# Seven of eight block products in half of the output projection of a two-layer decoder

## Chip, core and metric

One of the eight cores of a Trainium2 chip runs the whole program. The metric is device microseconds for one execution. A core has a matrix engine (TensorE, PE in the profile), three engines for elementwise work (VectorE or DVE, ScalarE or ACT, GpSimd or POOL) and a queue engine, SyncE (SP), which issues all DMAs of this kernel. Each engine works its own instruction list strictly in order and waits there for the others.

## What is computed

Two decoder layers on 1024 tokens with 1024 features, in float32, then a final norm. Cut to what matters here:

```python
def reference(x, ...):
    for l in range(2):
        h = rmsnorm(x, norm1[l])
        qa, ka, va, qb, kb, vb, gate_pre = split(h @ w_in[l])
        o_a = dilated_mixture(qa, ka, va)           # 12 heads of windowed attention
        o_b = stick_breaking_attention(qb, kb, vb)  # 4 heads
        gates = sigmoid(gate_pre + b_gate[l])
        merged = g_a * (o_a @ w_br[l, :256]) + g_b * (o_b @ w_br[l, 256:])
        x = x + merged @ w_o[l]                     # the output projection
        h2 = rmsnorm(x, norm2[l])
        a, v = split(h2 @ w_up[l])                  # 2 x 2816 columns
        a = causal_depthwise_conv(a, conv_w[l], conv_b[l])
        x = x + (gelu(a) * v) @ w_down[l]
    return rmsnorm(x, norm_f)
```

The stick-breaking attention takes for each query the product, over later keys, of (1 - sigmoid): a running product along a row of up to 1024 keys, which the kernel makes with a scan on DVE.

## The kernel before

**Layout and precision.** Activations lie with features on the 128 partitions and tokens along the free axis; the tokens come in two halves of 512, n = 0 and 1, the features in eight chunks of 128, e or k = 0 to 7. To keep float32 accuracy each operand is held as two numbers, hi and lo (`split`: ACT casts hi, L131, DVE subtracts to get lo, L136), and every block product is three matmuls: hi x hi, hi x lo, lo x hi. `product` (L163 to L165) does so for a whole chunk over eight k: 24 matmuls of 512 columns.

**Seven products.** The FFN's up and down projections, and the gates and far-attention inputs of the mixer, are already done in pairs of chunks by Winograd's form of Strassen's scheme: the input is a 2 by 2 grid of blocks (token half by feature half), the weights of two output chunks another, and seven block products of 12 matmuls (`seven`, L921 to L923) take the place of eight. It needs four sums of input blocks, S[1] to S[4], each split into hi and lo, and four sums of weight blocks per pair. For the mixer these come from `block_sums`, a list of small steps put between other work (`dense.side`), each of which waits for a named event such as "N01s".

**Order.** PE's order is that of the program text, written by hand through generators: a unit yields after a few matmuls, and `drive(side, main, ratio, lead)` runs `lead` steps of main and then `ratio` steps of main for each step of side. The other engines' orders and the DMA queue's are made by a planner from priorities and estimated times: it may pull an instruction ahead of its place in the text when its inputs and its buffer are there, and raises those in `tc.high_priority`. The buffers are named by tags: `ql` (2), `p4` (4), `e8` (6), `wr` (2, raw weights), `wh` and `wl` (4 each, split weights), `ot` (1), `pt` (6 of 512 columns).

**Around the change.** In the mixer stick-breaking items come first. `score` computes a row block, ACT takes two sigmoids of it, and `scans` runs the scan over the whole row (L651) and a multiplication (L654); it is called after each `turn`, which transposes 128-blocks on PE (L667) and splits them into `sbh` and `sbl`, read by `apply` (L679). The near items follow (`p0h`, `p0l`, L743), then the far items, with the pairs of `pair` between them. Then comes the branch loop: 16 steps over (n, e), each with two products of `product` into `br_ps`, a multiplication by the gate (L1297), their sum `mrg` (L1302), which `merged` writes into H[n] as hi (ACT) and lo (POOL). In the first layer this loop also transposes x into the residual (`residual_in`). The gates are loaded by `gate_in` (`gin`), the branch weights by `branch_in` through `wr`. Before this loop `next(wo[0])` loads and splits the weights of the first output chunk, through `wr` as well.

The output projection itself is 16 units `wo_chunk(l, n, e)`, all eight e for n = 0, then all for n = 1. Each loads its own weights, runs `product` into `o_ps`, adds the result to x (L1136) and its squares to the norm's sum (`norm_add`, L424, L426). `relay` makes each unit's weights ready one unit ahead. `drive(first_half(), relay(*wo, primed=True), 2.5, 36)` puts the second norm of half 0 (sums L473, factors L482, `hh` and `hl` L487 to L490) and the FFN's first input sum (`first_sum`, L463) between the chunks of n = 1. The norm of half 1 runs between the first products of the FFN (`u_ps`).

Of the kernel before, what the change touches and what calls it, by code (L numbers as in the profile page):

```python
# [56 lines left out]
def trunk_kernel(ctx, tc, x, norm1, w_in, b_gate, w_br, w_o, norm2, w_up, conv_w, conv_b, w_down, norm_f, out, depth=None, probe=None):  # L57
# [341 lines left out]
    def xc(n, e, sub=slice(0, HF)):  # L399
        return X[n][e // 4][:, e % 4, sub]  # L400
# [15 lines left out]

    def norm_add(n, e, first=False, sub=slice(0, HF), adds=None):

        if first:
            ACC[n] = sb.tile([P, HF], F32, tag="ql", bufs=2, name="nrm")  # L420
        acc = ACC[n]
        acc = acc[:, sub]
        sq = acc if first else small("sq")[:, sub]
        act.activation(sq, xc(n, e, sub), AF.Square)  # L424
        if not first:
            (adds or (dve if e % 3 == 1 else pool)).tensor_tensor(acc, acc, sq, ALU.add)  # L426
# [193 lines left out]
    def stick_item(pr, s, qp):  # L620
# [6 lines left out]
        def score(a):  # L627
# [6 lines left out]
            for c0 in range(0, L, 512):  # L634
# [3 lines left out]
                with tc.high_priority(offset=AHEAD):  # L638
# [3 lines left out]
                    act.activation(sv[:, c0 : c0 + w], z[:, :w], AF.Sigmoid, scale=-1.0)  # L642
            SCANS.append((bt, sv, L))
            if L <= 512:
                scans()

        def scans():

            for bt, sv, L in SCANS:
                rev = sv[:, 0:L][:, ::-1]  # L650
                one = dve.tensor_tensor_scan(rev, rev, zero[:, 0:1].to_broadcast([P, L]), 1.0, ALU.mult, ALU.add)  # L651
# [9 lines left out]
        def turn(kb):  # L661
# [6 lines left out]
            shared[kb] = parts(tp, len(todo) * P, "sb")  # L668
            scans()

# [256 lines left out]
    def block_sums():  # L927
# [16 lines left out]
        def further(t, a, i):  # L944
            if t == 4:

                S[4] = half(0, 0)
            elif i == 0:
                new_s(t)
            r, (ah, al) = keep["r"][:, i, :], a()[i]  # L950
# [33 lines left out]
    def pair(dense, l, offs, tiled, put):  # L984
# [29 lines left out]
        yield  # L1014
        pool.tensor_tensor(a11, a12, a11, ALU.subtract)
        yield
# [101 lines left out]
    def gate(l, c):  # L1118
# [4 lines left out]
        for n in range(2):  # L1123
# [5 lines left out]
            yield  # L1129

    def wo_chunk(l, n, e):
# [4 lines left out]
        dve.tensor_tensor(xc(n, e), xc(n, e), o, ALU.add)  # L1136
        norm_add(n, e, e == 0)
        yield

    def residual_in():  # L1140

        for n in range(2):
            for c in range(0 if n else 1, 4):
                xr = sb.tile([P, T], F32, tag="ql", bufs=2, name="xr")
                t0 = n * HF + c * P
# [8 lines left out]
    def mixer(l, pending):  # L1154
# [123 lines left out]
        for i, ab in order:  # L1278
# [23 lines left out]
            dve.tensor_tensor(m, gt[:, 0, :], gt[:, 1, :], ALU.add)  # L1302
            late.append((n, e, m))
            if len(late) > 1:
# [643 lines left out]
```

## Time and profile before

| | us |
|---|---|
| median of 3 runs (2694.21 to 2697.93) | 2696.02 |
| the profiled execution | 2700.21 |
| its span, first to last instruction | 2698.4 |
| PE busy | 2662.5 |
| DVE busy | 2017.0 |
| ACT busy | 1352.6 |
| POOL busy | 672.1 |
| mean granted TensorE clock | 0.997 |

The span is that of one execution; its own time is 1.8 us longer. Matmuls overlap in the array, so a busy PE says that it is never without a matmul, not how many it starts: that is seen in the number of instructions in a window. In the rows a time in brackets is the idle time of that engine ahead of the instruction, with what ended it. In the rows of windows each engine has its busy time and its count, and behind them stand the granted clock, the share of the DMA engines and GB/s.

### The profile page before, as it was taken

Reading aid. Unit: us, or ns where it says so; the run is one execution under the profiler, and the core shown is the slowest. Engines: PE = TensorE matmul, PEld = TensorE weight load, DVE = VectorE, ACT = ScalarE, POOL = GpSimd, SP = SyncE. Lnnn points to the kernel's source line nnn. Section 1 sums busy time; section 2 is a strip of 40 time slices with the busy share of each in tenths; the row PEclk is TensorE's granted clock in tenths of the full one; section 3 lists DMA queues with packets and bytes.
Section 4 is the critical chain, followed back from the end, with each engine's and each line's share of the span. In section 5 each row is a group of like instructions: output and inputs, shape, how many; then the busy total and the mean of one; then the engine's idle time right before and its main releaser. Section 6 shows DMA issues by size and latency. Waiting matters only on the chain.

```text
span 2698.4 us, 36609 instructions
## 1 busy us (share of the span) xinstructions
PE 2662.5 (99%) x13104; PEld 2233.0 (83%) x13104; DVE 2017.0 (75%) x2974; ACT 1352.6 (50%) x2494; POOL 672.1 (25%) x487
## 2 busy tenths in 40 slices
PE   9999999999999999999999999999999999999999
PEld 8988888878888888888888888888788888888888
DVE  5776855675788888897657777566858888898865
ACT  5655645474455555532435565455645555554225
POOL 1003221122233444321210042211211443343210
PEclk9999999999999999999999999999999999999999
DMA  5012178663234444688411122785732444446863
GB/s 161 28 56 85 57 189 247 199 231 105 82 124 166 146 151 150 222 319 319 161 36 43 48 79 87 210 247 177 233 89 76 156 156 141 164 149 252 330 248 120
DMA packets 358689, 421.03 MB, mean 156 GB/s; under 512 B 20732, under 2 KB 287340, under 8 KB 356972
## 3 DMA queue, kind: packets, MB, share of 16 engines
q1 hardware_dynamic: 358508, 418.70, 47.0%
q8 instruction: 103, 1.69, 0.3%
q14 instruction: 78, 0.64, 0.1%
HBM read 278.59 MB, written 140.05 MB: 155 GB/s over the span
## 4 chain that ended last, share of the span: by engine, by line
PE 84%; DVE 8%; issue 2%; ACT 2%; DMA 2%; POOL 0%; SPq 0%; DVEq 0%; ACTq 0%; POOLq 0%
PE u_a L921 5%; PE u_a L922 5%; PE u_a L923 5%; PE d_ps L1644 5%; PE d_ps L1645 5%; PE d_ps L1646 5%; PE u_c L921 3%; PE u_c L922 3%; PE u_c L923 3%; PE i_a L921 2%; PE i_a L922 2%; PE i_a L923 2%; PE o_ps L163 2%; PE o_ps L164 2%; PE o_ps L165 2%
## 5 line engine op out<-in xcount | busy, mean ns | idle before, releaser
L136 DVE TENSOR_TENSOR w_lo<-up_a,w_hi 128x512 fp32r<-128x512 f32 x240 | 237.6, 996 | 20.6 <-ACT w_hi L131 20.6
L131 ACT CAST w_hi<-up_a 128x512 fp32r<-128x512 f32 x240 | 149.3, 622 | 184.1 <-PE u_a L922 45.3
L1652 DVE TENSOR_TENSOR x<-x,d_ps 128x512 f32<-128x512 f32 (+1 forms) x228 | 151.8, 671 | 76.6 <-PE d_ps L1646 75.3
L1383 POOL TENSOR_TENSOR cv<-cv 128x512 f32<-128x512 f32 x88 | 132.3, 1515 | 249.3 <-DVE cv L1378 139.5
L136 DVE TENSOR_TENSOR w_lo<-w_raw,w_hi 128x512 fp32r<-128x512 f32 x148 | 111.6, 757 | 61.9 <-ACT w_hi L131 61.3
L136 DVE TENSOR_TENSOR g<-cv,g 128x512 fp32r<-128x512 f32 x154 | 152.6, 992 | 5.2 <-ACT g L131 2.7
L131 ACT CAST w_hi<-w_raw 128x512 fp32r<-128x512 f32 x148 | 91.9, 621 | 125.3 <-PE o_ps L164 64.3
L131 ACT CAST w_hi<-in_a 128x512 fp32r<-128x512 f32 x120 | 74.6, 621 | 121.1 <-PE i_c L922 53.6
L136 DVE TENSOR_TENSOR w_lo<-in_a,w_hi 128x512 fp32r<-128x512 f32 x120 | 86.8, 723 | 61.9 <-ACT w_hi L131 61.5
L1644 PE MATMUL d_ps<-gd_in,w_hi 128*128 128x512 f32 (+1 forms) x340 | 130.4, 384 | 1.7 <-issue 0.9
L1646 PE MATMUL d_ps<-gd_in,w_lo 128*128 128x512 f32 (+1 forms) x340 | 129.8, 382 | 0.0
L1645 PE MATMUL d_ps<-gd_in,w_hi 128*128 128x512 f32 (+1 forms) x340 | 129.8, 382 | 0.0
L921 PE MATMUL u_a<-hh,w_hi 128*128 128x512 f32 x320 | 124.6, 389 | 0.8 <-DVE u L1534 0.8
L922 PE MATMUL u_a<-t_lo,w_hi 128*128 128x512 f32 x320 | 124.5, 389 | 0.0
L922 PE MATMUL u_a<-hl,w_hi 128*128 128x512 f32 x320 | 124.5, 389 | 0.0
L923 PE MATMUL u_a<-hh,w_lo 128*128 128x512 f32 x320 | 124.5, 389 | 0.0
L921 PE MATMUL u_a<-t_hi,w_hi 128*128 128x512 f32 x320 | 124.5, 389 | 0.0
L923 PE MATMUL u_a<-t_hi,w_lo 128*128 128x512 f32 x320 | 124.5, 389 | 0.0
L1644 PE MATMUL d_ps<-gd_in,wd 128*128 128x512 f32 (+1 forms) x292 | 113.9, 390 | 0.0
L131 ACT CAST g<-cv 128x512 fp32r<-128x512 f32 x154 | 94.9, 616 | 37.2 <-POOL cv L1383 29.9
L1646 PE MATMUL d_ps<-gd_in,wd 128*128 128x512 f32 (+1 forms) x292 | 112.8, 386 | 0.0
L1645 PE MATMUL d_ps<-gd_in,wd 128*128 128x512 f32 (+1 forms) x292 | 112.8, 386 | 0.0
(404 smaller groups left out, 8606.7 us busy)
## 6 DMA issues: line engine op xcount, KB each, us to landing
gd<-g SPq DMA_DIRECT2D x154, 512.0 KB, 3.7
gd_in<-gd SPq DMA_DIRECT2D x154, 512.0 KB, 5.9
up_a<-in_w_up_dram SPq DMA_DIRECT2D x80, 512.0 KB, 4.9
t_kq<-tk SPq DMA_DIRECT2D x32, 768.0 KB, 4.7
wd_raw<-in_w_down_dram SPq DMA_DIRECT2D x22, 1024.0 KB, 11.8
w_raw<-in_w_in_dram SPq DMA_DIRECT2D x80, 256.0 KB, 3.0
in_a<-in_w_in_dram SPq DMA_DIRECT2D x40, 512.0 KB, 5.4
gin<-gs SPq DMA_DIRECT2D x32, 512.0 KB, 4.1
```

The costliest lines, as they stand in the source:

```text
L131: one = act.copy(hi, src)
L136: two = dve.tensor_tensor(lo, src, f32(hi), ALU.subtract)
L163: pe.matmul(o, lh, rh, start=(first and i == 0), stop=False, skip_group_check=share)
L164: pe.matmul(o, lh, rl, start=False, stop=False, skip_group_check=share)
L921: pe.matmul(o, w[0][:, c], rh, start=(first and i == 0), stop=False, skip_group_check=True)
L922: pe.matmul(o, w[0][:, c], rl, start=False, stop=False, skip_group_check=True)
L923: pe.matmul(o, w[1][:, c], rh, start=False, stop=(last and i == 3), skip_group_check=True)
L1383: return lambda: pool.tensor_tensor(dst, a, b, ALU.subtract)
L1644: pe.matmul(o[:, sub], wh[:, c], gh[:, sub], start=(i == 0 and k in (0, 4, 5)), stop=False, skip_group_check=True)
L1645: pe.matmul(o[:, sub], wh[:, c], gl[:, sub], start=False, stop=False, skip_group_check=True)
L1646: pe.matmul(o[:, sub], wl[:, c], gh[:, sub], start=False, stop=(i == m - 1), skip_group_check=True)
L1652: dve.tensor_tensor(x, x, o[:, sub], ALU.add)
```

## The change

Output chunks 0 to 3 are computed in two pairs, (0, 1) and (2, 3), for both halves at once with seven block products (`wo_pair`); chunks 4 to 7 stay plain. The order is: chunks 4 to 7 of half 0, the two pairs, chunks 4 to 7 of half 1. The four input sums of the merged branches are made by `merged_sums`: the first, r = m(0, e) - m(1, e), on POOL in the branch loop, S[1], S[2] and S[3] with DVE and ACT, S[4] with POOL and ACT in the place of H[0]'s first half. `wo_all` sets them between the steps of the chunks by a count of steps, and makes each unit's weights ready during the one before. The second norm of half 0 now runs between the four plain chunks of half 1 (lead 44, ratio 1.2).

The first chunk's weights are loaded at step i == 12 of the branch loop instead of ahead of it. The scans of the stick-breaking rows go in pieces of at most 512 columns, from the end of the row to its start, each beginning with the last value of the one before; after a turn all but two of the waiting pieces are done, at least one. In `block_sums` the subtraction of b22 moves from the series after "N11s" to one after "N01s". In `pair` the difference a12 - a11 moves from POOL to DVE. x tiles of the first layer's residual go alternately to `ot` and `ql`, and the norm's sums to `ot` (half 1) and `p4` (half 0).

```diff
-        def scans():
-            for bt, sv, L in SCANS:
-                rev = sv[:, 0:L][:, ::-1]
-                one = dve.tensor_tensor_scan(rev, rev, zero..., 1.0, ALU.mult, ALU.add)
+            for c1 in range(L, 0, -512):
+                SCANS.append((bt, sv, max(0, c1 - 512), c1, L))
+        def scans(most=9):
+            while SCANS and most:
+                most -= 1
+                bt, sv, c0, c1, L = SCANS.pop(0)
+                rev = sv[:, c0:c1][:, ::-1]
+                one = dve.tensor_tensor_scan(rev, rev, zero..., 1.0 if c1 == L else sv[:, c1 : c1 + 1], ALU.mult, ALU.add)
...
-                dve.tensor_tensor(bt[:, 0 : L - 1], bt[:, 0 : L - 1], sv[:, 1:L], ALU.mult)
-            SCANS.clear()
+                k0, k1 = max(0, c0 - 1), c1 - 1
+                dve.tensor_tensor(bt[:, k0:k1], bt[:, k0:k1], sv[:, k0 + 1 : k1 + 1], ALU.mult)
...
-            scans()
+            scans(max(1, len(SCANS) - 2))
...
-        series({"N11s"}, 2, lambda i: further(2, b22, i), 1, 1)
+        for i in range(4):
+            todo.append(({"N01s"}, lambda i=i: less(b22, i)))
+        series({"N11s"}, 2, lambda i: i or new_s(2), 0, 1)
...
-        pool.tensor_tensor(a11, a12, a11, ALU.subtract)
+        dve.tensor_tensor(a11, a12, a11, ALU.subtract)
...
+    def wo_pair(l, e):
+        def put(c, n, x):
+            wo_add(n, e + c, x, n == 1 and e + c == 0)
...
+        u1, u2 = u[:, HF:T], u[:, 0:HF]
+        with tc.high_priority(offset=AHEAD):
+            pool.tensor_tensor(u2, a11, a21, ALU.subtract)
+            SUMS.append(pool.tensor_tensor(a21, a21, a22, ALU.add).ins.name)
+        yield
+        w1 = piece(a11)
+        yield
+        w2 = piece(a12)
+        yield
+        dve.tensor_tensor(a11, a21, a11, ALU.subtract)
+        w6 = piece(a11)
+        yield
+        w5 = piece(a21)
+        yield
+        pool.tensor_tensor(a11, a12, a11, ALU.subtract)
...
+        yield from seven(pa, w1, half(1, 0), True, True)
+        act.copy(u1, pa)
+        w7 = piece(u2)
+        yield
+        yield from seven(pb, w2, half(1, 1), True, True)
+        dve.tensor_tensor(u1, u1, pb, ALU.add)
+        put(0, 1, u1)
+        w3 = piece(a11)
+        yield
+        yield from seven(pa, w6, S[2], False, True)
...
+        yield from seven(pc, w5, S[1], True, True)
+        act.copy(u5, pc)
+        w4 = piece(a22)
...
+        yield from seven(pa, w7, S[3], False, True)
+        dve.tensor_tensor(u5, u5, pa, ALU.add)
+        put(1, 0, u5)
...
+        yield from seven(pc, w3, half(0, 1), False, True)
+        dve.tensor_tensor(u2, u2, pc, ALU.add)
+        put(0, 0, u2)
...
+        for word in seven(pa, w4, S[4], False, True):
+            yield "turn"
+            yield
+        put(1, 1, pa)
...
+    def merged_sums(r):
+        b12, b21, b22 = half(0, 0), half(1, 1), half(0, 1)
...
+        def s1(i):
+            split(*S[1][i], r[:, i, :])
+        def s2(i):
+            dve.tensor_tensor(r[:, i, :], f32(b22[i][0]), r[:, i, :], ALU.subtract)
+            dve.tensor_tensor(r[:, i, :], r[:, i, :], f32(b22[i][1]), ALU.add)
+            split(*S[2][i], r[:, i, :])
+        def s3(i):
+            t = small("s3")
+            dve.tensor_tensor(t, f32(b22[i][1]), f32(b12[i][1]), ALU.subtract)
+            dve.tensor_tensor(t, t, f32(b22[i][0]), ALU.add)
+            dve.tensor_tensor(t, t, f32(b12[i][0]), ALU.subtract)
+            split(*S[3][i], t)
+        def s4(i):
+            one = pool.tensor_tensor(r[:, i, :], f32(b21[i][0]), r[:, i, :], ALU.subtract)
+            tc.add_manual_dep(one.ins, SUMS[-1], NO_SYNC, reason="behind the sums of weights")
+            pool.tensor_tensor(r[:, i, :], r[:, i, :], f32(b21[i][1]), ALU.add)
+        def s4_parts(i):
+            act.copy(S[4][i][0], r[:, i, :])
+            pool.tensor_tensor(S[4][i][1], r[:, i, :], f32(S[4][i][0]), ALU.subtract)
+        for i in range(4):
+            at(i, lambda i=i: s1(i))
+            at(4 + i, lambda i=i: s2(i))
+            at(14 + 2 * i, lambda i=i: s3(i))
+            at(16 + 2 * i, lambda i=i: s4(i))
+            at(23 + i, lambda i=i: s4_parts(i))
...
-        wo = [wo_chunk(l, n, e) for n in range(2) for e in range(KD)]
+        wo = [(wo_chunk(l, 0, e), 1) for e in range(4, KD)] + [(wo_pair(l, e), READY) for e in (0, 2)]
+        wo += [(wo_chunk(l, 1, e), 1) for e in range(4, KD)]
...
-        next(wo[0])
         next(residual, None)
...
+                    pool.tensor_tensor(r1[0][:, e, :], mrg.pop((0, e)), mrg.pop((1, e)), ALU.subtract)
...
+            if i == 12:
+                next(wo[0][0])
...
-        drive(first_half(), relay(*wo, primed=True), 2.5, 36)
+        drive(first_half(), wo_all(wo[0], wo[1:], merged_sums(r1[0])), 1.2, 44)
```

`wo_all` goes through the units in this order; at each step of the running unit it does the sums due at that count, and at each step of a chunk or "turn" of a pair it advances the weights of the next unit by one. The first pair's weight load and block sums go ahead at counts 0 and 2.

More of the change, by code (lines that the diff above doesn't have):

```diff
@@ L415, in trunk_kernel, with norm_add @@
     ACC = [None, None]
-    def norm_add(n, e, first=False, sub=slice(0, HF), adds=None):
+    def norm_add(n, e, first=False, sub=slice(0, HF), adds=None, place=None):
         if first:
-            ACC[n] = sb.tile([P, HF], F32, tag="ql", bufs=2, name="nrm")
+            ACC[n] = sb.tile([P, HF], F32, **(place or dict(tag="ql", bufs=2)), name="nrm")
         acc = ACC[n]
@@ L947, in further, with less @@
                 S[4] = half(0, 0)
-            elif i == 0:
-                new_s(t)
+            less(a, i)
+        def less(a, i):
             r, (ah, al) = keep["r"][:, i, :], a()[i]
@@ L1129, in gate, with wo_add @@
             yield
+    def wo_add(n, e, y, first):
+        dve.tensor_tensor(xc(n, e), xc(n, e), y, ALU.add)
+        norm_add(n, e, first, place=dict(tag="ot") if n else dict(tag="p4", bufs=4))
     def wo_chunk(l, n, e):
@@ new lines, in wo_all @@
+    def wo_all(first, rest, todo):
+        units = [first] + rest
+        count, early = 0, next(u for u in rest if u[1] > 1)
+        todo.setdefault(0, []).insert(0, lambda: next(early[0]))
+        todo.setdefault(2, []).insert(0, lambda: next(early[0]))
+        for i, (u, n) in enumerate(units):
+            then, left = units[i + 1] if i + 1 < len(units) else (None, 0)
+            if then is early[0]:
+                left -= 2
+            for word in u:
+                if word == "turn" or n == 1:
+                    if left:
+                        next(then)
+                        left -= 1
+                if word != "turn":
+                    for f in todo.get(count, ()):
+                        f()
+                    count += 1
+                    yield
+            while left:
+                next(then)
+                left -= 1
@@ L1143, in residual_in @@
             for c in range(0 if n else 1, 4):
-                xr = sb.tile([P, T], F32, tag="ql", bufs=2, name="xr")
+                xr = sb.tile([P, T], F32, **(dict(tag="ot") if c % 2 else dict(tag="ql", bufs=2)), name="xr")
                 t0 = n * HF + c * P
```

51 lines of the change are left out of this document (47 added, 4 removed).

## The prediction

> **What bounds the kernel now.** I read the page first, then windows over the stages, then who made TensorE wait, and last the timeline around the longest waits.
>
> ```profile
> span 2698.4 us, 36609 instructions
> PE 2662.5 (99%) x13104; PEld 2233.0 (83%) x13104; DVE 2017.0 (75%) x2974; ACT 1352.6 (50%) x2494; POOL 672.1 (25%) x487
> PE 84%; DVE 8%; issue 2%; ACT 2%; DMA 2%; POOL 0%; SPq 0%; DVEq 0%; ACTq 0%; POOLq 0%
> ...
> 860.00:1110.00 250.00, 250.00 (x1105) 207.01 (x1104) 221.46 (x245) 129.46 (x204) 96.62 (x65) 1.00 0.44 151
> 626.00:714.00 88.00, 88.00 (x396) 72.99 (x395) 47.16 (x69) 35.49 (x59) 19.34 (x13) 1.00 0.32 93
> 570.00:626.00 56.00, 53.48 (x256) 43.78 (x255) 43.77 (x60) 40.90 (x70) 20.29 (x15) 0.97 0.66 223
> ```
>
> The first three lines are the page's: TensorE is busy for 99% and holds 84% of the chain. In the windows (columns PE, PEld, DVE, ACT, POOL) the FFN stage starts 1105 matmuls in 250 us, one each 0.226 us, without a gap; that is the price of a 512-column matmul. The first layer's output projection (626 to 714) is as tight on PE, while DVE stands at 47 of 88 us. The branch stage ahead of it (570 to 626) loses 2.5 us and some clock (0.97). So a removed matmul is worth 0.226 us as long as nothing else becomes late, and the other place for a gain is what PE still waits for:
>
> ```profile
> PE br_ps L163 <- DVE gin L1297: 8.0, 4, 3.7
> PE sb_o L679 <- DVE sbl L136: 4.3, 4, 1.7
> PE o L743 <- DVE p0l L136: 2.7, 3, 1.2
> PE z L599 <- DVE st L826: 2.4, 3, 1.4
> PE u_ps L164 <- DVE hl L490: 1.3, 2, 0.7
> ```
>
> Each row is the sum over both layers, the times, the longest. Four of the five are in stages that the change touches.
>
> **The matmuls.**
>
> ```profile
> L163 PE MATMUL o_ps<-hh,w_hi 128*128 128x512 f32 x256 | 100.0, 391 | 0.0
> ```
>
> 256 on this line of the three of `product` means 128 a layer and 24 matmuls for each of 16 chunks. Afterwards eight chunks stay (192) and two pairs take seven products of 12 (168): 360 for 384 a layer, 48 fewer in all, 48 x 0.226 = **-10.9 us**.
>
> **The later weights.** Layer two, 1904 to 1911:
>
> ```profile
> 1904.02 1.05 DVE L903 TENSOR_TENSOR on<-on,jn 128x512 f32<-128x512 f32 x1
> ...
> 1905.99 0.39 PE L165 MATMUL br_ps<-oh_b,br_w 128*128 128x512 f32 x1
> 1906.92 0.62 ACT L131 CAST w_hi<-w_raw 128x512 fp32r<-128x512 f32 x1 [5.55 <-DMA w_raw<-in_w_o_dram]
> 1907.57 0.69 DVE L136 TENSOR_TENSOR w_lo<-w_raw,w_hi 128x512 fp32r<-128x512 f32 x1 [2.50 <-ACT w_hi L131]
> 1908.70 0.69 DVE L136 TENSOR_TENSOR ol_a<-on,oh_a 128x512 fp32r<-128x512 f32 x1 [0.43 <-ACT oh_a L131]
> 1909.31 1.28 DVE L1297 TENSOR_TENSOR gin<-gin,br_ps 128x512 f32<-128x512 f32 x2
> 1910.05 0.50 PE L163 MATMUL br_ps<-oh_b,br_w 128*128 128x512 f32 x1 [3.66 <-DVE gin L1297]
> 1910.95 0.63 PE L163 MATMUL br_ps<-oh_b,br_w 128*128 128x512 f32 x1
> ...
> 1913.51 0.63 PE L163 MATMUL br_ps<-oh_a,br_w 128*128 128x512 f32 x1
> ```
>
> ACT stands 5.55 us before the cast of the first w_o chunk, because its load is late; DVE stands behind that cast, and the gate product that frees PE's bank stands behind both. From 1905.99 to 1910.05 PE starts nothing: 4.06 less 0.226 = 3.8 us lost. Then a clock drop: seven matmuls from 1910.95 to 1913.51 last 0.63 instead of 0.39 and start every 0.43, 0.2 us more each, 1.4. Together 5.2. Layer one is the same thing at one remove:
>
> ```profile
> 566.09 0.69 DVE L136 TENSOR_TENSOR w_lo<-w_raw,w_hi 128x512 fp32r<-128x512 f32 x1 [1.18 <-ACT w_hi L131]
> 566.80 0.37 SPq L1250 DMA_DIRECT2D br_raw<-in_w_br_dram  x1
> 570.46 1.14 ACT L131 CAST br_w<-br_raw 128x512 fp32r<-128x512 f32 x2 [2.02 <-DMA br_raw<-in_w_br_dram]
> 574.61 0.50 PE L163 MATMUL br_ps<-oh_b,br_w 128*128 128x512 f32 x1 [2.52 <-DVE gin L1297]
> ```
>
> The w_o pieces hold both `wr` buffers, so the branch weights are issued at 566.80, as soon as `w_lo` has let one go, and ACT waits for them. That costs 2.5 and a drop as above, 3.9. The diff moves that load to i == 12 of the branch loop, so both waits lose their cause. What is late next is the chain of the join: L903 ends at 1905.07, then cast 0.62, `ol_a` 0.69, gate 0.69, PE free at 1907.1, about 1 us after it wants to go. 5.2 + 3.9 less two times 1.0 is 7.1; I take **-7.0**. Below, the bound is -9.1; above it is 0, if at i == 12 ACT is held in the same way, or if the x tile that now waits for `ot` in SP's queue (behind it: the gate loads) makes layer one keep its wait. The four new r = m0 - m1 on POOL I cost at nothing there: POOL has 20.3 of 56 us.
>
> **Scans in pieces, sums of h moved.**
>
> ```profile
> L651 DVE TENSOR_TENSOR_SCAN stay<-stay,zero 128x1024 f32<-128x1024 f32 x8 | 18.3, 2284 | 1.1 <-ACT stay L642 1.1
> L651 DVE TENSOR_TENSOR_SCAN stay<-stay,zero 128x512 f32<-128x512 f32 x8 | 9.8, 1225 | 1.1 <-ACT stay L642 1.0
> ```
>
> A 1024 scan is 2.28 us on DVE, two of 512 are 2.45: 0.17 more in sum, but the longest block ahead of the `sbl` that PE waits for is halved. I take half of the 4.3: -2.2. Of the h sums, eight DVE operations leave the crowd around the first far-attention units, where `p0l` is late; half of 2.7 is -1.3. In the pairs a12 - a11 goes from POOL to DVE, one operation for each of 20 pairs in a stage in which PE waits for little: 0, at most the 1.4 of one more wait like that at `z`. In sum **-3.5**, bounds -7.0 (all of both) and +3 (pieces that fall in front of another split, as large as today's `z` waits).
>
> **The new sums.** They are the price: S1 4 splits, S2 8 operations and 4 splits, S3 12 and 4, all on DVE, S4 8 and 4 operations on POOL. Prices:
>
> ```profile
> 667.60 0.69 DVE L1136 TENSOR_TENSOR x<-x,o_ps 128x512 f32<-128x512 f32 x1 [1.56 <-PE o_ps L165]
> 668.20 0.69 DVE L136 TENSOR_TENSOR w_lo<-w_raw,w_hi 128x512 fp32r<-128x512 f32 x1
> ...
> 284.66 1.67 DVE L951 TENSOR_TENSOR h_sum<-hh,h_sum 128x512 f32<-128x512 f32 x1
> 286.36 1.66 DVE L952 TENSOR_TENSOR h_sum<-h_sum,hl 128x512 f32<-128x512 f32 x1
> ...
> 244.56 1.30 POOL L938 TENSOR_TENSOR h_sum<-hl 128x512 f32<-128x512 f32 x1 [15.80 <-PE sb_o L679]
> 285.85 1.62 POOL L942 TENSOR_TENSOR h_sum<-h_sum,hh 128x512 f32<-128x512 f32 x1
> ...
> 589.88 0.38 SPq L148 DMA_DIRECT2D w_raw<-in_w_o_dram  x1
> ```
>
> DVE alone goes on every 0.60 us (667.60 to 668.20). Beside POOL it takes turns: 1.70 from 284.66 to 286.36 for one DVE and one POOL operation, where POOL alone needs 1.30. The last row is the load of the second chunk, 36 us before that stage: ready work is pulled ahead. The time: four chunks (24 x 0.226 = 5.4 each) and four products (2.7 each) are 32.6 us until product five reads S3, 34.6 until its last block. DVE has to do by then: splits for chunks 6 and 7 (4), six splits and a difference of the pair (7), S1 4, S2 12, S3 16, and 3 for a merge, a norm sum and x; 46, and 5 adds from PSUM. If 9 of the 12 plain S3 operations are pulled into the branch stage (DVE 43.8 of 56 us there), 37 stay. POOL has 13 in that time: 2 left merges, 2 norm sums, 1 difference, 8 of S4. 13 x 1.70 + 24 x 0.60 + 1.5 (half of the PSUM adds hidden) = 38.0, 3.4 too late; I take 3.5 a layer, **+7.0**. Bounds: all 12 pulled ahead and S4 behind S3: 5 x 1.70 + 29 x 0.60 + 1.5 = 27.4, cost 0; nothing pulled ahead and 15 POOL operations: 15 x 1.70 + 31 x 0.60 + 3 = 47.1, 12.5 late. Products 6 and 7 then hide S4.
>
> The Trainium skill's page "SBUF — State Buffer", section "Who interferes with whom", says that a DVE instruction with two SBUF inputs and a GpSimd instruction that reads SBUF exclude each other for the whole instruction. The trace agrees nearly: 1.70 where the full exclusion would give 0.60 + 1.30 = 1.90. By the rule the stall would be 13 x 0.2 = 2.6 us a layer longer and the whole change 5.2 us worse, 2690.4; it speaks against putting S4 on POOL.
>
> **The end of the stage.** Half of norm 0's cover goes: before, eight chunks (43 us) followed the last half-0 chunk, now four (21.7) follow the pairs.
>
> ```profile
> L426 POOL TENSOR_TENSOR nrm<-nrm,sq 128x512 f32<-128x512 f32 x29 | 40.2, 1385 | 264.3 <-ACT sq L424 263.6 <-DVE nrm L426 0.7
> L424 ACT ACTIVATE sq<-x 128x512 f32<-128x512 f32 x52 | 32.7, 630 | 25.4 <-DVE x L1652 18.6 <-DVE x L1136 6.7
> L463 DVE TENSOR_TENSOR s<-b_f,b_f 128x512 f32<-128x512 f32 x8 | 5.5, 689 | 0.0
> ```
>
> From product six to the norm's sums PE has product seven and one step, 18 x 0.226 = 4.1 us. The chain needs two adds (0.69 each), square 0.63, POOL sum 1.39 and a last matmul's 0.39: 3.8. I give 0.5 a layer for queueing, 0 to 2. The first sum of the FFN (4 x 0.69 and its splits) has one of four steps done before the FFN today, afterwards hardly any; two DVE operations more, 1.3 us, fall on the `hl` wait of 0.7. 1.8 a layer, **+3.6**, bounds 0 and 12 (2 + 4 a layer). Weight loads fall from 16 chunks to 12 a layer: no gain, DMA is at 0.32.
>
> **Sum.** -10.9 - 7.0 - 3.5 + 7.0 + 3.6 = -10.8. The profiled execution took 2700.2 us (span 2698.4, 1.8 around it), 4.2 above the median of 2696.0. 2700.2 - 10.8 = 2689.4; against the median **2685.2**.
>
> **Rivals.** (1) The sums are late and decide: nothing is pulled ahead and S4 runs against S3. 12.5 us a layer and the clock drop after such a wait (1.4) are 27.8 instead of 7.0: -10.8 + 20.8 = +10.0, 2706.0, slower. For it: the alternation at 284.66, and that the whole of S1 to S3 follows one sum, r. Against: the load at 589.88, and DVE's 47 of 88 us. It cancels the change from 8.9 us a layer on (3.5 + 10.8 / 2). (2) The branch wait moves instead of going, and the scans give nothing: -10.9 + 7.0 + 3.6 = -0.3, 2695.7. For it: two loads, not one, were late in that stage; against: both hang on the same `wr` buffers. (3) The sums are hidden wholly and the end costs 0.5 a layer: -10.9 - 7.0 - 3.5 + 1.0 = -20.4, 2675.6.
>
> **How the numbers follow.** Forecast 0.42, (1) 0.20, (2) 0.16, (3) 0.22. About 0.2% (5.4 us, 2690.6 to 2701.4) can be told from no change. Faster: most of the forecast (0.39), (3) and little of (2): 0.62. Same: the rest of the forecast, most of (2) and a part of (1): 0.19. Slower: 0.19. Low end beyond (3), toward the bound of the branch and scan terms: 2670. High end at (1): 2706. The forecast's own range is 2680 to 2691.
>
> **What would show it.** 720 matmuls in the stage over both layers: `product` with o_ps 128 a line instead of 256 and 112 new ones a line in `seven`. Right if `br_ps` waits for `gin` under 3 us in sum and no w_o cast stands between L903 and the gates; if `sb_o` waits about 2; if in the first pair PE waits some 3 us for a t_lo or t_hi and in the second pair for nothing; if `u_ps` and `nrm_t` together wait 1 to 3 us a layer. Wrong if the first pair waits 9 us a layer or more (1), or if the 8.0 stands in the table again under another releaser (2).

## The result: 2722.9 us, slower by 1%

| | before | after |
|---|---|---|
| median, us (4 runs each) | 2696.97 (2694.21 to 2698.39) | 2722.87 (2721.16 to 2724.80) |
| profiled execution, us | 2700.21 | 2724.80 |

The ratio is 1.0097, with a 95% interval of 1.0080 to 1.0115. Faster by 10.8 us was predicted; it is slower by about 26 and lies above the range. First the page of the changed kernel: span, the row of the engines, the chain that ended last.

```profile
span 2723.0 us, 36653 instructions
PE 2667.8 (98%) x13056; PEld 2232.0 (82%) x13056; DVE 2114.6 (78%) x3132; ACT 1370.4 (50%) x2534; POOL 722.9 (27%) x513
PE 81%; DVE 11%; issue 2%; DMA 2%; ACT 2%; POOL 0%; DVEq 0%; ACTq 0%; POOLq 0%; SPq 0%
```

The 48 matmuls are gone (13104 to 13056). But DVE is busy for 97.6 us more, POOL for 50.8, and DVE's share of the chain went from 8 to 11%. The stretches between PE's landmarks (the first matmul into each bank, read from the timeline) say where, layer one / layer two, in us:

| from the first ... to the first ... | before | after | difference |
|---|---|---|---|
| `sb_t`, `i_a`: stick and near items | 247.5 / 247.3 | 245.6 / 245.3 | -1.9 / -2.0 |
| `i_a`, `br_ps`: pairs, far items | 248.6 / 249.0 | 245.8 / 246.5 | -2.8 / -2.5 |
| `br_ps`, `o_ps`: branch stage | 54.7 / 52.0 | 51.6 / 47.4 | -3.1 / -4.6 |
| `o_ps`, `u_ps`: output projection | 88.5 / 88.5 | 104.2 / 101.0 | +15.7 / +12.5 |
| `u_ps`, `u_a`: norm 1, start of the FFN | 46.5 / 46.5 | 53.2 / 53.7 | +6.7 / +7.3 |

So 16.9 us are won ahead of the output projection and 42.2 lost in it and behind it. What PE waited for in the changed kernel (sum, times, longest, over both layers):

```profile
PE i_a L925 <- ACT u L1190: 11.9, 2, 6.0
PE nrm_t L473 <- DVE nrm L426: 8.3, 3, 4.5
PE i_a L925 <- ACT t_hi L131: 5.2, 2, 2.6
...
PE o_ps L163 <- ACT t_hi L131: 2.4, 2, 1.5
PE br_ps L163 <- DVE gin L1456: 2.3, 4, 1.2
PE i_a L925 <- DVE x L1139: 2.2, 2, 1.1
PE nrm_t L473 <- POOL nrm L426: 1.9, 3, 0.9
```

`sb_o` and `o` at `p0l` have left the table, `br_ps` fell from 8.0 to 2.3. In their place stand waits inside the pairs (`i_a`) and at norm 1 (`nrm_t`). The windows of the first layer (columns PE, PEld, DVE, ACT, POOL, then the clock): the whole output projection, its first 37 us, and the branch stage ahead of it.

```profile
616.10:720.30 104.20, 91.42 (x374) 72.17 (x373) 89.48 (x106) 44.57 (x79) 56.52 (x34) 0.93 0.15 44
616.10:653.20 37.10, 28.51 (x121) 22.02 (x119) 36.61 (x38) 15.09 (x27) 30.84 (x17) 0.98 0.20 57
564.50:616.10 51.60, 50.91 (x249) 41.49 (x248) 44.06 (x58) 38.55 (x68) 23.30 (x17) 1.00 0.83 273
```

In the first 37 us DVE has hardly a gap: 38 operations in 36.6 us, 0.96 each, beside 17 on POOL. The branch stage runs 58 operations on DVE; over the same stage (569.2 to 623.9) it was 59 before. The timeline around the longest wait shows the rest:

```profile
640.93 0.68 DVE L1139 TENSOR_TENSOR x<-x,o_ps 128x512 f32<-128x512 f32 x1
...
642.62 1.77 DVE L1248 TENSOR_TENSOR s<-hl 128x512 f32<-128x512 f32 x1
643.80 1.74 POOL L1254 TENSOR_TENSOR m_sum<-hh,m_sum 128x512 f32<-128x512 f32 x1
644.42 1.66 DVE L1249 TENSOR_TENSOR s<-s,hh 128x512 f32<-128x512 f32 x1
645.50 1.73 POOL L426 TENSOR_TENSOR nrm<-nrm,sq 128x512 f32<-128x512 f32 x1
646.12 1.66 DVE L1250 TENSOR_TENSOR s<-s,hh 128x512 f32<-128x512 f32 x1
647.19 1.71 POOL L1256 TENSOR_TENSOR m_sum<-m_sum,hl 128x512 f32<-128x512 f32 x1
647.70 1.75 DVE L136 TENSOR_TENSOR w_lo<-o_a,w_hi 128x512 fp32r<-128x512 f32 x1
647.81 0.62 ACT L131 CAST t_hi<-s 128x512 fp32r<-128x512 f32 x1 [4.97 <-DVE s L1250]
...
651.05 0.68 DVE L1139 TENSOR_TENSOR x<-x,o_ps 128x512 f32<-128x512 f32 x1
651.76 0.63 ACT L424 ACTIVATE sq<-x 128x512 f32<-128x512 f32 x1 [2.29 <-DVE x L1139]
652.80 0.58 ACT L1190 COPY u<-i_a 128x512 f32<-128x512 f32 x1
653.43 0.80 PE L925 MATMUL i_a<-t_hi,w_hi 128*128 128x512 f32 x1 [5.96 <-ACT u L1190]
654.03 0.63 PE L926 MATMUL i_a<-t_lo,w_hi 128*128 128x512 f32 x1
```

642.62 is the first of S3's 12 differences in this layer: none was pulled into the branch stage, while S4, which is needed last, is in POOL's hands from 630 on. The first block of S3 takes three DVE operations of 1.66 to 1.77 us each, in turn with POOL, where 0.60 is DVE's pace alone. What PE's wait ends with is not even S3: it is the bank of product one, which product three uses again. The copy that frees it (L1190) stands in ACT's list behind the cast of S3's first block, for which ACT stood 4.97 us, and behind a square for which it stood 2.29 more. The bank is not the only late thing: by the kernel's order the `w_lo` of 647.70 is the lo part of product three's own weights, which DVE made behind the three differences, and it is there at 649.45, 2 us after the last matmul of product two. Behind the wait the clock drops: a matmul now lasts 0.63.

The end of the stage on DVE, layer one:

```profile
718.81 2.99 DVE L463 TENSOR_TENSOR s<-b_f,b_f 128x512 f32<-128x512 f32 x3
721.72 1.88 DVE L136 TENSOR_TENSOR t_lo<-s,t_hi 128x512 fp32r<-128x512 f32 x3
723.53 0.68 DVE L136 TENSOR_TENSOR w_lo<-w_raw,w_hi 128x512 fp32r<-128x512 f32 x1
724.13 0.67 DVE L1139 TENSOR_TENSOR x<-x,o_ps 128x512 f32<-128x512 f32 x1
724.73 0.68 DVE L136 TENSOR_TENSOR w_lo<-w_raw,w_hi 128x512 fp32r<-128x512 f32 x1
725.33 0.68 DVE L463 TENSOR_TENSOR s<-b_f,b_f 128x512 f32<-128x512 f32 x1
725.93 0.68 DVE L426 TENSOR_TENSOR nrm<-nrm,sq 128x512 f32<-128x512 f32 x1
```

`o_ps` ends at about 720.5, its add to x runs at 724.13: the differences and splits of `first_sum` stand ahead of it. The last square's sum comes at 725.93, and PE, which has done its first 12 `u_ps` matmuls, waits for it (`nrm_t`), at the cost of another clock drop.

### The profile page after: what moved, and what is told of

The parts are those of the page before. It is cut to its first block, busy times and chain, and to the rows that moved or that the text cites. A ratio compares the mean times of both kernels' runs of the same rounds, so it can differ in the third digit from the quotient of the medians.

```text
span 2723.0 us, 36653 instructions
## 1 busy us (share of the span) xinstructions
PE 2667.8 (98%) x13056; PEld 2232.0 (82%) x13056; DVE 2114.6 (78%) x3132; ACT 1370.4 (50%) x2534; POOL 722.9 (27%) x513
## 4 chain that ended last, share of the span: by engine, by line
PE 81%; DVE 11%; issue 2%; DMA 2%; ACT 2%; POOL 0%; DVEq 0%; ACTq 0%; POOLq 0%; SPq 0%
PE u_a L925 5%; PE u_a L926 5%; PE u_a L927 5%; PE d_ps L1811 5%; PE d_ps L1813 5%; PE d_ps L1812 5%; PE i_a L925 3%; PE i_a L926 3%; PE i_a L927 3%; PE u_c L927 2%; PE u_c L925 2%; PE u_c L926 2%; DVE w_lo L136 2%; PE g_ps L163 2%; PE g_ps L165 2%
## 5 line engine op out<-in xcount | busy, mean ns | idle before, releaser
L131 ACT CAST w_hi<-in_a 128x512 fp32r<-128x512 f32 x120 | 74.6, 621 | 118.2 <-PE i_c L926 51.6
L1012 POOL TENSOR_TENSOR u<-in_a 128x512 f32<-128x512 f32 x20 | 27.5, 1375 | 346.9 <-DMA tk<-u 134.4
L136 DVE TENSOR_TENSOR w_lo<-w_raw,w_hi 128x512 fp32r<-128x512 f32 x116 | 96.1, 832 | 29.5 <-ACT w_hi L131 29.2
L655 DVE TENSOR_TENSOR_SCAN stay<-stay,zero 128x512 f32<-128x512 f32 (+2 forms) x96 | 93.5, 974 | 28.8 <-ACT stay L642 28.2
L1811 PE MATMUL d_ps<-gd_in,wd 128*128 128x512 f32 (+1 forms) x292 | 113.9, 390 | 0.0
L1813 PE MATMUL d_ps<-gd_in,wd 128*128 128x512 f32 (+1 forms) x292 | 112.8, 386 | 0.0
```

The lines of the kernel that those rows point to most:

```text
L131: one = act.copy(hi, src)
L136: two = dve.tensor_tensor(lo, src, f32(hi), ALU.subtract)
L1811: pe.matmul(o[:, sub], wh[:, c], gh[:, sub], start=(i == 0 and k in (0, 4, 5)), stop=False, skip_group_check=True)
L1813: pe.matmul(o[:, sub], wl[:, c], gh[:, sub], start=False, stop=(i == m - 1), skip_group_check=True)
```

## Experiments

### The edits without the pairs, and the pairs without their sums

`e1_plain_rest`: all edits but the pairs; 16 chunks as before.

```diff
-        norm_add(n, e, first, place=dict(tag="ot") if n else dict(tag="p4", bufs=4))
+        norm_add(n, e, first)
...
-        wo = [(wo_chunk(l, 0, e), 1) for e in range(4, KD)] + [(wo_pair(l, e), READY) for e in (0, 2)]
...
+        wo = [wo_chunk(l, n, e) for n in range(2) for e in range(KD)]
...
-        drive(first_half(), wo_all(wo[0], wo[1:], merged_sums(r1[0])), 1.2, 44)
+        drive(first_half(), relay(*wo, primed=True), 2.5, 36)
```

> All edits kept (later weights, scans in pieces, sums of h moved, the difference on DVE), the output projection as before: 16 chunks of 24 matmuls. Theory (what was lost was lost to the pairs and their sums, nothing else of the change costs): the two output projections are back at 88.5 us each and the stretch from the first u_ps to the first u_a at 46.5, and the gains ahead of them stay: 2697.0 - 16.9 = about 2680. Rival (the FFN's start lost its 7 us a layer because first_sum and the moved buffers come late, not because of the pairs): the u_ps stretch stays at 53 and the time is about 2694.

Measured: 2682.27 us, ratio to before 0.9945 (0.9929 to 0.9962). The output projections take 88.5 in both layers, the stretch behind them 46.5. The theory's numbers hold. The rival is not decided by this: the edit also puts back the norm sums' buffers and the old order of `first_half`, so that `first_sum` is no longer late here either. e12 and e15, below, show that the place of `first_sum` is most of that loss. This is the fastest version of the study and beats both kernels.

`e3_no_sums`: the pairs as they are, S1 to S4 left out.

```diff
+        S.update({1: half(1, 0), 2: half(1, 1), 3: b22, 4: b12})
-        for i in range(4):
+        for i in range(0):
             at(i, lambda i=i: s1(i))
...
-                    pool.tensor_tensor(r1[0][:, e, :], mrg.pop((0, e)), mrg.pop((1, e)), ALU.subtract)
+                    if e == 0:
+                        pool.tensor_tensor(r1[0][:, e, :], mrg.pop((0, e)), mrg.pop((1, e)), ALU.subtract)
```

> S1 to S4 are left out: products three to seven read blocks of the merged branches that exist already, and of the four differences r only one is made. The pairs' own work (sums and splits of weights, adds of the products) stays. Theory (the sums of the merged branches are the price): the output projection takes 360/2 = 180 x 2 x 0.226 = 81.4 us a layer and 1 or 2 us of waits, the u_ps stretch 47: 2697 - 16.9 - 10.9 + 4 = about 2673. Rival (the pairs' own sums, splits and adds saturate DVE too): half of the 42 us of loss stays, about 2693.

Measured: 2687.99 us, ratio 0.9966 (0.9953 to 0.9979). Its window of the first output projection:

```profile
616.40:701.30 84.90, 83.63 (x374) 68.72 (x373) 58.77 (x76) 37.29 (x65) 28.19 (x21) 1.00 0.19 54
```

84.9 and 84.8 us, against 83.0 for 88.5 less 24 matmuls: the pairs alone cost 1.8 a layer, 1.3 of it in waits (0.7 for the copy L1190, 0.6 at `nrm_t`), so the sums of the merged branches are the price of this stage, as the theory had it. But the stretch behind stayed at 53.0 and 54.0, where the theory had 47, and so the time is nearer to the rival's 2693 than to 2673: the loss at the FFN's start does not need S1 to S4. Against e1, pairs without any sums win 3.6 us a layer in the stage: that is all that the sums may cost.

### What the sums cost, and on which engine

`e2_s4_dve`: S4's 12 operations a layer on DVE.

```diff
-            one = pool.tensor_tensor(r[:, i, :], f32(b21[i][0]), r[:, i, :], ALU.subtract)
-            tc.add_manual_dep(one.ins, SUMS[-1], NO_SYNC, reason="behind the sums of weights")
-            pool.tensor_tensor(r[:, i, :], r[:, i, :], f32(b21[i][1]), ALU.add)
+            dve.tensor_tensor(r[:, i, :], f32(b21[i][0]), r[:, i, :], ALU.subtract)
+            dve.tensor_tensor(r[:, i, :], r[:, i, :], f32(b21[i][1]), ALU.add)
...
-            pool.tensor_tensor(S[4][i][1], r[:, i, :], f32(S[4][i][0]), ALU.subtract)
+            dve.tensor_tensor(S[4][i][1], r[:, i, :], f32(S[4][i][0]), ALU.subtract)
```

> The 12 operations a layer of S4 go from POOL to DVE. Theory (while POOL runs, each DVE operation with two SBUF inputs lasts 1.7 instead of 0.6, so a POOL operation costs DVE about 1.1 us): DVE loses 12 x 1.1 = 13 us of slowing and gains 12 x 0.65 = 8 us of work a layer; the output projection falls from 104.2 and 101.0 by about 5 each, the time to about 2713. Rival (DVE has too many operations, whoever runs beside it): 8 us a layer more, about 2738.

Measured: 2711.49 us, ratio 1.0055 (1.0040 to 1.0070), with output projections of 95.1 and 96.0. Window of the first:

```profile
617.20:712.30 95.10, 86.61 (x374) 69.53 (x373) 85.31 (x116) 43.24 (x76) 34.72 (x22) 0.98 0.17 48
```

DVE runs ten operations more than in the changed kernel (116 for 106) and is busy for 4.2 us less; the stage is 9.1 us shorter (5.0 in layer two), where about 5 each were expected. The theory holds. The rival, too many operations on DVE whoever runs beside it, is out as the explanation of S4.

`e13_no_s4`: S4 left out.

```diff
-            at(16 + 2 * i, lambda i=i: s4(i))
-            at(23 + i, lambda i=i: s4_parts(i))
+        S[4] = b12
```

> The changed kernel with S4's 12 POOL operations and 4 casts left out (the last product reads a block of the merged branches that exists). The output projections take 104.2 and 101.0 with S4 on POOL, 95.1 and 96.0 with it on DVE. Theory (S4 costs on either engine, on DVE 12 x 0.6, on POOL 12 x 1.1 or more through the sharing): 88 to 89 each, so that POOL's price is 12 to 16 a layer and DVE's 7; the time about 2695. Rival (on DVE S4 fell behind product five and cost nothing): 94 to 96 each, 2710.

Measured: 2704.65 us, ratio 1.0041 (1.0026 to 1.0056); 91.6 and 91.2 us, between the two expectations. In the mean of the layers S4 costs 95.5 - 91.4 = 4.1 us on DVE and 102.6 - 91.4 = 11.1 on POOL: 0.34 and 0.93 for each of the 12 operations. The direction of the theory is right; its price for POOL (12 to 16) was slightly too high, that for DVE (7) by 2.9.

`e10_no_s3` and `e9_s4_dve_no_s3`: S3's 12 differences left out, with S4 on POOL and on DVE.

```diff
-            dve.tensor_tensor(t, f32(b22[i][1]), f32(b12[i][1]), ALU.subtract)
-            dve.tensor_tensor(t, t, f32(b22[i][0]), ALU.add)
-            dve.tensor_tensor(t, t, f32(b12[i][0]), ALU.subtract)
-            split(*S[3][i], t)
+            split(*S[3][i], f32(b22[i][0]))
```

> The changed kernel, S4 on POOL as it is there, without S3's 12 plain differences. Theory (a DVE operation with two SBUF inputs beside a running POOL costs 1.7): six to twelve of them stand in POOL's stretch, so 12 to 18 us a layer less, but not below the 88 of the run without S3 on DVE alone; the output projections go from 104.2 and 101.0 to about 90, the time to about 2698. Rival (the alternation is of no account, an operation costs 0.6): 7 a layer, 97 and 94, about 2709.

Measured: 2718.11 us, ratio 1.0087 (1.0070 to 1.0104); 97.6 us in both layers, 6.5 and 3.4 less. The theory's 90 is out. Layer one is the rival's number, but layer two gains half of it, and the time is 9 us above the rival's 2709. The reason is in the waits:

```profile
PE i_a L925 <- DVE x L1139: 12.2, 2, 6.1
PE nrm_t L473 <- DVE nrm L426: 7.4, 3, 3.6
PE i_a L925 <- ACT u L1199: 3.2, 2, 1.7
```

The 6 us wait did not go: it moved from the copy in front of product three to an x add in front of product one, which DVE was late with. With S4 on POOL some operation of DVE is 6 us late either way; which one PE meets is a matter of order. With S4 on DVE and the same differences left out (next run) the longest such wait is 3.4.

> S4 on DVE, and the 12 plain differences of S3 left out (its split reads a block of the merged branches as it is). With S4 on DVE the output projections take 95.1 and 96.0, without any sums 84.9. Theory (the sums are paid in DVE time one for one, none of them was pulled ahead): 12 x 0.6 = 7.2 a layer less, about 88.3 each, the time about 2697. Rival (S3 was hidden, S1 and S2 are what PE waits for): under 2 a layer, 2708.

Measured: 2705.23 us, ratio 1.0035 (1.0022 to 1.0048); 92.1 and 92.9 us, 3.0 and 3.1 less than with S3. Neither: S3's differences were not hidden, and they cost 0.26 each and not 0.6.

`e14_s4_dve_no_s1_s2`: S4 on DVE, S1 and S2 left out.

```diff
-            at(i, lambda i=i: s1(i))
-            at(4 + i, lambda i=i: s2(i))
+        S.update({1: half(1, 0), 2: b21})
```

> S4 on DVE, S1 and S2 left out (products three and four read blocks that exist): 8 differences and 8 splits a layer less. With all sums there 95.1 and 96.0, without S3's differences 92.1 and 92.9, without any 84.9. Theory (DVE time, operation by operation): 16 x 0.6 = 9.6 less casts that were waited for, but not below 85 to 87; the time about 2693. Rival (S3, whose splits stand last, decides alone): under 3 a layer, 2706.

Measured: 2707.14 us, ratio 1.0044 (1.0028 to 1.0060); 91.3 and 93.6 us, 3.7 and 2.3 less. Again about 3 a layer, close to the rival's bound, but S3 doesn't decide alone either: leaving out S3's differences, or S1 and S2, or S4 saves 3.1, 3.0 and 4.1, and leaving out all saves 10.7. No single sum decides. They add up.

`e6_two_ahead`: S4 on DVE, `first_sum` later, and two chunks of half 1 ahead of the pairs.

```diff
+        late_ = [(wo_chunk(l, 1, e), 1) for e in range(4, KD)]
+        wo = wo[:4] + late_[:2] + wo[4:] + late_[2:]
...
-        drive(first_half(), wo_all(...), 1.2, 44)
+        drive(first_half(), wo_all(...), 1.2, 52)
```

> S4 on DVE and first_sum later, and two of the four half-1 chunks moved ahead of the two pairs (main loop's lead 52 for 44): 10.8 us more for the sums of the merged branches, 10.8 us less cover for norm 0. Theory (the sums are late, not too many): the output projections go from 95.1 and 96.0 with S4 on DVE to about 86, and with the u_ps stretch at 47 to 50 the time is about 2680. Rival (DVE is short over the whole stage): the stalls stay, 94 or more each, about 2697; or norm 0 has too little cover and u_ps waits 5 us or more a layer.

Measured: 2711.24 us, ratio 1.0058 (1.0043 to 1.0073); output projections of 92.0 and 91.6, behind them 48.7 and 48.7. With 10.8 us more time the stage gains 3.7, not 10. Neither expectation fits: a third of what the sums cost is gone, and the stage is not at 94. The two halves of the first layer's stage (the same columns) say where DVE is short:

```profile
617.20:664.00 46.80, 42.63 (x182) 33.43 (x181) 46.58 (x64) 22.20 (x40) 14.93 (x9) 1.00 0.24 68
664.00:709.20 45.20, 42.95 (x193) 34.72 (x192) 34.04 (x47) 19.69 (x36) 16.38 (x12) 1.00 0.10 29
```

DVE is full up to 664 and has 11 us of room behind it. So it is not short over the whole stage, as the rival had it, but until the middle of the first pair, where the sums, the splits of the weights and the adds stand in one list. The wait at `u_a` of the next experiment is in this time as well. Even here the stage is 3.3 us longer than 16 plain chunks.

### The end of the stage

`e5_first_sum_later` puts `first_sum` ahead of the FFN's own sums, `e12_first_sum_last` right behind the last chunk, `e15_no_first_sum` leaves it out.

```diff
             yield from norm(0, g2[:, 0, :], "t", keep=True)
-            yield from first_sum()
         drive(first_half(), wo_all(...), 1.2, 44)
+        for _ in first_sum():          # e12; in e5 it heads sums() of the FFN
+            pass
...
+            S[3] = half(0, 0)          # e15, in first_half in the place of first_sum
```

> The kernel after with one edit: first_sum (four differences and four splits) no longer follows norm 0 in first_half but stands ahead of the FFN's own sums. Theory (three differences and three splits of first_sum stand on DVE ahead of the last x add, so that norm 1's sums come 3.75 us late and the clock drops for ten matmuls behind it): the stretch from the first u_ps to the first u_a goes from 53.2 and 53.7 back to 46.5 to 47, 14 us in all, about 2709. Rival (norm 1 is late because the half-1 sums of squares themselves now crowd the end): the stretch stays above 51, 2719 or more.

Measured: 2729.45 us, ratio 1.0121 (1.0104 to 1.0138). The stretch behind the output projection fell to 47.3 and 48.4, but the one after it grew from 381.3 to 389.0 (388.8 in layer two). From the waits:

```profile
PE u_a L927 <- DVE w_lo L136: 10.5, 2, 5.3
...
PE nrm_t L473 <- DVE nrm L426: 2.9, 3, 1.9
```

The cause was right in the main, the remedy was not: the same DVE work now stands in front of the first pair of the FFN.

> The changed kernel with first_sum right behind the last chunk of the output projection, ahead of norm 1, not beside the last chunks. Theory (it stands on DVE ahead of the last x add and makes norm 1 late): the stretch from the first u_ps to the first u_a goes from 53.2 and 53.7 to 47 or 48, without the new wait of 5.3 at u_a that its place among the FFN's sums brought: about 2711. Rival (norm 1 is late by the crowd of sums of squares): above 51, 2718 or more.

Measured: 2718.14 us, ratio 1.0086 (1.0071 to 1.0101); 48.8 and 51.5 us, no new wait at `u_a`, `nrm_t` at 4.0. In between: 4.3 and 2.3 of the 7 come back; layer two and the time are the rival's.

> The changed kernel with first_sum left out (the FFN's first products read a block of h that exists). Its later places left 47.3 and 48.4 or 48.8 and 51.5 us between the first u_ps and the first u_a, where the changed kernel has 53.2 and 53.7 and the kernel before 46.5. Theory (first_sum ahead of the last x add is the whole of it): 46.5 to 47.5 in both layers, about 2710. Rival (the sums of squares crowd the end as well): 48.5 or more in at least one.

Measured: 2716.38 us, ratio 1.0078 (1.0060 to 1.0096); 47.4 and 50.0 us, `nrm_t` still at 3.0. By its own bound the rival has a part: `first_sum` is 5.8 and 3.8 of the loss. The rest (0.9 and 3.5) is left for the shorter cover and the sums of squares, which no run separates.

### The edits ahead of the output projection

`e4_late_only`: the kernel before, the first `w_o` weights at i == 12.

```diff
-        next(wo[0])
         next(residual, None)
...
+            if i == 12:
+                next(wo[0])
```

> The kernel before with one edit: the weights of the first w_o chunk are loaded and split from i == 12 of the branch loop on, not ahead of it. Theory (the late load and the casts behind it made br_ps wait): the branch stages go from 54.7 and 52.0 to 51.6 and 47.4, 7.7 us in sum, about 2689. Rival (the branch stage gained because the work ahead of it was done earlier by the other edits): under 3 us, 2694 to 2697.

Measured: 2691.27 us, ratio 0.9982 (0.9972 to 0.9991), 2.4 to 7.5 us faster. Branch stages 50.6 and 46.4: 4.1 and 5.6 us shorter, but the far items of layer two grew by 2.5.

`e7_scans_only`, `e8_less_only` and `e11_a12_dve`: the kernel before with the scans in pieces, the sums of h moved, a12 - a11 on DVE.

```diff
+            for c1 in range(L, 0, -512):                                   # e7
+                SCANS.append((bt, sv, max(0, c1 - 512), c1, L))
...
+        for i in range(4):                                                 # e8
+            todo.append(({"N01s"}, lambda i=i: less(b22, i)))
...
-        pool.tensor_tensor(a11, a12, a11, ALU.subtract)                    # e11
+        dve.tensor_tensor(a11, a12, a11, ALU.subtract)
```

> The kernel before with the scans in pieces alone. The kernel with all edits but the pairs gained 13.4 us, the later weights alone 4.4 to 8.6 of it. Theory (the long scans delayed sbl): the stretch from the first sb_t to the first i_a goes from 247.5 and 247.3 to 245.6 and 245.3, nothing else moves: about 2692. Rival (these 3.8 us come from the h sums moved): under 1 us.

Measured: 2694.65 us, ratio 0.9993 (0.9983 to 1.0002). The stick stretch is 245.6 and 245.3: -1.9 and -2.0, all of it due to the scans, as expected. But the pairs and far items took back 2.0 and 1.3.

> The kernel before with the sums of h moved alone (the eight DVE operations of the second sum done right after N01s, a12 - a11 left on POOL). Theory (they crowd the far attention's first units where p0l is late): the stretch from the first i_a to the first br_ps goes from 248.6 and 249.0 to 247.3 and 247.6, half of the 4.8 us that the whole change gains there, the rest being a12 - a11: about 2694. Rivals: all of the 4.8 is theirs (2691), or none (2696).

Measured: 2694.25 us, ratio 0.9996 (0.9987 to 1.0005). Pairs and far items -0.5 and 0.0: nearly nothing.

> The kernel before with a12 - a11 alone on DVE instead of POOL. Scans alone moved the stretch from the first i_a to the first br_ps by +2.0 and +1.3, the sums of h alone by -0.5 and 0.0, all edits together by -2.3 and -2.4. Theory (a12 - a11 on POOL slowed DVE's splits beside it): this edit alone gives most of it, -2 a layer, about 2692. Rival (it takes the edits together, a wait that moves unless all its causes go): within 0.7 a layer, 2696.

Measured: 2692.41 us, ratio 0.9991 (0.9980 to 1.0001). Pairs and far items -1.9 and -1.4: most of what the theory asked for, the largest share of the three, and alone none of the three can be told from no change by its time. In e1 the same stretch gains 2.3 and 2.4 with all of them, though the three alone sum to -0.4 and -0.1: the effects do not simply add up.

In layer two the branch stage of these three is 47.6, 47.7 and 48.1, against 52.0 before, with the `w_o` load at its old place. So there the 3.66 us wait goes with any shift of what is ahead. Whether every execution of the kernel before has it stays open: its profiled execution took 2700.2 us, 3 to 5 more than the medians.

## Why the prediction was wrong, step by step

- **Matmuls, -10.9: right as a count, short as time.** 48 fewer are on the page. The pairs alone brought 3.6 a layer, 7.2, since 1.8 a layer went to two short waits and what follows them (e3).
- **Later weights, -7.0: right, within the measured interval.** In the profile the branch stages lost 7.7, `br_ps` waits 2.3 in sum (under 3 was asked), and the edit alone gives 4.9 by the ratio, 2.4 to 7.5. In layer two other edits remove the wait as well.
- **Scans, sums of h, a12 - a11, -3.5: right in sign, too small.** In the profile -3.9 for the scans and -5.3 in pairs and far items; by medians e1 less e4, 9.0. The term that was mis-sized is a12 - a11, costed at nothing; alone it gives 3.3 in that stretch (e11). That POOL's operation slowed DVE's splits there, as S4 does later, fits but is only argued. `sb_o` and `p0l` went to nothing, where a half was expected to stay.
- **New sums, +7.0: this step failed.** It measured 104.2 + 101.0 - 2 x 83.0 = 39.2, less 3.6 for the pairs' own waits: 35.6. Two assumptions broke. That "9 of the 12 plain S3 operations are pulled into the branch stage": none was; the row of the second chunk's load, which the prediction used as evidence, is a DMA, and told nothing of DVE, which is busy for 44 us of 52 there, beside 23 of POOL. And that the lateness counts only from product five on and ends there: the wait at product five did come (2.6 us a layer, 3.5 was booked), but 6.0 more fell on product three, through ACT's list, and 1.1 on product one. POOL ran 17 operations in the first 37 us where 13 had been counted. Rival (1) had the mechanism (nothing pulled ahead, S4 against S3, the price of alternation), and its sign: "wrong if the first pair waits 9 us a layer or more", and the rows of `i_a`, all in the first pair, are 1.1 + 6.0 + 2.6 = 9.7. Its upper bound, 12.5 a layer and 1.4 for the clock, was 3.9 a layer short of 17.8, and not by the waits: PE waits 12.6 and 11.4 us in the stage, 1.3 in e3, so 10.7 a layer for the sums. It allowed one clock drop a layer; three came in layer one and two in layer two. 23 and 16 matmuls start some 0.43 us after the one before instead of 0.226, some 4 us a layer, and the first layer's stage has a granted clock of 0.93 where e3 has 1.00. The rest, some 3 a layer, lies in the first matmuls behind the waits, which start 0.3 to 0.7 us apart.
- **End of stage, +3.6: wrong by 10.** It measured 14.0. The chain of norm 0 that was counted is fine (`nrm_t` waits 0.9 there at most); norm 1 was not. The "1.3 us on the `hl` wait of 0.7" fell elsewhere: that wait is unchanged, and `first_sum` with its splits stands ahead of the last x add, which is most of the loss (e12, e15); a clock drop follows. The step that failed is the wait that was counted: norm 0's, and not norm 1's.
- **The rule weighed in the prediction.** The Trainium skill's page "SBUF — State Buffer", section "Who interferes with whom", says that a DVE instruction with two SBUF inputs and a GpSimd instruction that reads SBUF, here those of S4, exclude each other for the whole instruction. The rows agree nearly: from 642.62 on three such operations start 1.80 and 1.70 us apart where 0.60 is the pace alone and full exclusion would make it 1.90, and S4 is 7.0 us a layer dearer on POOL than on DVE. The rule spoke against this change. The 5.2 us that the prediction set against it were only the step from 1.70 to 1.90: the alternation itself stood in its sum (13 x 1.70), and what S4 would cost on DVE was not asked.

What is left open: the order in which the planner would have to place S3 and S4 so that DVE has room ahead of the first reader. No version with the pairs that was run comes below the plain one with the other edits, 2682.3.

## What to carry to other kernels

Trade matmuls for sums only where DVE and POOL have room together: count operations with two SBUF inputs on both engines as one queue, up to the first reader and not over the whole stage, and don't book work into an earlier stage without seeing the idle time there. For every wait that a late operation can cause, look at what stands behind it in its reader's list: here a cast that waited for a difference held up the copy that frees PE's bank. And before moving side work beside the last chunks, ask which operation ends last there, and what is put ahead of it.

## What the runs showed of the hardware that was not expected

Beside a running POOL operation, a DVE operation with one input from PSUM keeps its pace: L1139 took 0.68 at 640.93 and at 651.05, where the operations with two SBUF inputs from 642.62 to 649.38 took 1.66 to 1.77. The Trainium skill's page "SBUF — State Buffer" says in the same section that a DVE instruction with at most one SBUF input does not contend; the trace agrees. Whether moving an operand to PSUM would have saved the sums was not tried.

Which of the two engines is held up changed with what stood in DVE's list:

```profile
630.07 5.28 POOL L1254 TENSOR_TENSOR m_sum<-hh,m_sum 128x512 f32<-128x512 f32 x1 [4.24 <-DVE t_lo L136]
630.52 1.28 DVE L1240 TENSOR_TENSOR m_sum<-hh,m_sum 128x512 f32<-128x512 f32 x2
631.72 1.28 DVE L1241 TENSOR_TENSOR m_sum<-m_sum,hl 128x512 f32<-128x512 f32 x2
...
634.13 0.68 DVE L1139 TENSOR_TENSOR x<-x,o_ps 128x512 f32<-128x512 f32 x1
...
635.82 1.78 DVE L136 TENSOR_TENSOR w_lo<-w_raw,w_hi 128x512 fp32r<-128x512 f32 x1
```

S4's first operation on POOL stands in the record for 5.28 us while DVE goes on every 0.60 with operations of two SBUF inputs. It ends 1.22 us after the start of L1139, DVE's first operation since then with an input from PSUM, and 1.30 is what a POOL operation of this size takes alone; from 635.82 on the two take turns. Layer two shows the same (5.27 us from 1973.72, L1139 at 1977.78). So a dense run of DVE held POOL up, and not the other way round; that the PSUM input is what let POOL in is read from these rows, and no run tested it.
